# Issuing the first two stores of a streamed elementwise kernel from SyncE instead of GpSimd

## Chip, cores, metric

One core of one Trainium2 chip. The metric is the device time of one execution in microseconds (us), median of several executions. A ratio is the mean time of one kernel's runs over the mean of the other's runs in the same rounds on the same chip, so it is not quite the ratio of the medians that are quoted.

## The reference

```python
# pred, target: (8192, 8192) float32; target is 0.0 or 1.0
def reference(pred, target):
    eps = 1e-7
    pred = np.clip(pred, eps, 1 - eps)
    return -(target * np.log(pred) + (1 - target) * np.log(1 - pred))
```

Two inputs of 268 MB are read and one output of 268 MB is written. As target is 0 or 1, the kernel computes -ln|pred - 1 + target|, one Ln in place of two.

## The kernel before

The inputs are cut into chunks. Per partition there are two of 7680 elements, 32 of 15360, two of 7680 and one of 2048. Two rings in SBUF, one for pred (fp32, worked on in place and stored from there) and one for target (cast to bf16 while it is loaded), hold two large chunks each; chunk 3 lies where chunks 0 and 1 lay. So the load of pred for chunk 3 must wait until the stores of chunks 0 and 1 have landed.

I write pK, tK and sK for the load of pred, the load of target and the store of chunk K. Each of these is 128 rows, one per partition: the 16 DMA engines take 8 rows each. A transfer has landed when the last of its rows is through and its semaphore is up. A transfer that is issued and still waits for the DMA engines is backlog; a stretch in which nothing waits and the DMA engines stand idle is a hole.

```python
    def load(k):
        queue = nc.sync if k == 0 else nc.gpsimd
        nc.gpsimd.dma_start(out=spot(ring_t, k), in_=chunk(target, k))
        queue.dma_start(out=spot(ring_p, k), in_=chunk(pred, k))

    def store(k):
        queue = nc.sync if k >= n - 3 else nc.gpsimd
        queue.dma_start(out=chunk(out, k), in_=spot(ring_p, k))

    def front(k, *part):        # clamp, subtract-and-add on DVE; Abs, Ln on ACT
        ...
    def back(k, *part):         # multiply by -1 on DVE
        ...

        for k in range(3):
            load(k)
        ...
        front(0)
        front(1)
        back(0)
        store(0)
        back(1)
        store(1)
        load(3)
        for k in range(2, n - 4):
            front(k, (0, 2))
            front(k, (1, 2))
            back(k, (0, 2))
            back(k, (1, 2))
            store(k)
            for j in range(k + 2, n if k == n - 5 else k + 3):
                load(j)
        ...   # the last four chunks
```

## Time and profile before

| | before |
|---|---|
| median time | 1866.37 us (3 runs, 1865.87 to 1866.57) |
| span of the profiled run | 1864.1 us |
| DVE, ACT, GpSimd busy | 60%, 48%, 3% |
| DMA engines busy | 100%, nearly all for the GpSimd queue |
| bytes across HBM | 805 MB, 432 GB/s over the span |

How to read it: where the DMA engines are full from end to end and the bytes are fixed, only two things can change the time. One is time in which a DMA engine has nothing to do, the other is rows that take longer than they need. An idle engine elsewhere is not a loss.

### The profile page before, as it was taken

The page shows a single profiled execution, that of the slowest core. Times are in us where ns is not written, and L with a number is a line of the kernel's source. Part 1 is how long each engine was busy: PE and PEld are TensorE (multiplying, and loading weights), DVE is VectorE, ACT ScalarE, POOL GpSimd, SP SyncE. Part 2 cuts the span into 40 slices and gives each one's busy share as a digit, 9 for nine tenths or more (in the row PEclk, how much of TensorE's full clock was granted, in tenths as well). Part 3 has the DMA queues.
Part 4 walks back from the last instruction along what each step waited for, and adds up shares of the span by engine and source line. Part 5 has one row for each costly group of instructions (what it writes and reads, how often), then busy time and mean ns, then how long its engine had stood idle before and what let it go on. Part 6 is the DMA issues. An engine that isn't in the chain of part 4 may idle for free.

```text
span 1864.1 us, 619 instructions
## 1 busy us (share of the span) xinstructions
DVE 1122.2 (60%) x210; ACT 899.9 (48%) x142; POOL 57.5 (3%) x111
## 2 busy tenths in 40 slices
DVE  4655766555576655557665555766555576655585
ACT  3345553335555333555533355553335555333565
POOL 0000000000000000000000000000000000000000
DMA  9999999999999999999999999999999999999999
GB/s 295 374 357 341 353 343 368 383 384 351 347 352 344 371 382 384 348 349 353 347 367 384 382 352 347 353 345 368 385 382 352 345 353 348 365 387 380 353 334 389
DMA packets 15988, 671.13 MB, mean 360 GB/s; under 512 B 1776, under 2 KB 1776, under 8 KB 1904
## 3 DMA queue, kind: packets, MB, share of 16 engines
q0 software_dynamic: 15408, 658.25, 98.5%
q1 hardware_dynamic: 576, 12.85, 1.7%
q14 instruction: 4, 0.03, 0.0%
HBM read 536.87 MB, written 268.44 MB: 432 GB/s over the span
## 4 chain that ended last, share of the span: by engine, by line
DMA 35%; issue 26%; ACT 22%; DVE 15%; POOL 1%; DVEq 0%; POOLq 0%; PEldq 0%
DMA ring_p<-in_pred_dram 32%; ACT ring_p L88 11%; ACT ring_p L89 11%; DVE ring_p L85 7%; DVE ring_p L82 4%; DVE ring_p L93 4%; DMA out_dram<-ring_p 3%; POOL ring_t L73 0%; POOL out_dram L78 0%; DVEq L157 0%; POOL ring_p L74 0%; POOLq L78 0%; POOLq L73 0%; DVEq L82 0%; PEldq L157 0%
## 5 line engine op out<-in xcount | busy, mean ns | idle before, releaser
L88 ACT ACTIVATE ring_p<-ring_p 128x7680 f32<-128x7680 f32 (+1 forms) x70 | 450.6, 6437 | 941.4 <-DVE ring_p L85 941.4
L85 DVE SCALAR_TENSOR_TENSOR ring_p<-ring_t,ring_p 128x7680 f32<-128x7680 bf16 (+1 forms) x70 | 557.2, 7960 | 2.4
L82 DVE TENSOR_SCALAR ring_p<-ring_p 128x7680 f32<-128x7680 f32 (+1 forms) x70 | 284.0, 4057 | 399.0 <-DMA ring_p<-in_pred_dram 399.0
L93 DVE TENSOR_SCALAR ring_p<-ring_p 128x7680 f32<-128x7680 f32 (+1 forms) x69 | 284.0, 4117 | 321.5 <-ACT ring_p L89 321.5
L89 ACT ACTIVATE ring_p<-ring_p 128x7680 f32<-128x7680 f32 (+1 forms) x70 | 451.1, 6444 | 2.2
L74 POOL DMA_DIRECT2D ring_p<-in_pred_dram x36 | 19.3, 535 | 909.2 <-DMA out_dram<-ring_p 909.2
L78 POOL DMA_DIRECT2D out_dram<-ring_p x34 | 18.2, 537 | 851.0 <-DVE ring_p L93 851.0
L73 POOL DMA_DIRECT2D ring_t<-in_target_dram x37 | 20.3, 550 | 0.8 <-PEq L157 0.8
L99 ACT ACT_TABLE_LOAD x1 | 1.3, 1283 | 0.7 <-PEq L146 0.7
L96 DVE MEMSET warm<- 1x8 f32 x1 | 0.1, 65 | 0.8 <-PEq L146 0.8
L99 ACT ACTIVATE warm<-warm 1x8 f32<-1x8 f32 x1 | 0.2, 208 | 0.0
L146 POOL MEMSET const-float32-0.0<- 128x1 f32 x1 | 0.1, 98 | 0.2 <-issue 0.2
L146 POOL MEMSET const-bfloat16-1.0<- 128x1 bf16 x1 | 0.1, 101 | 0.0
L146 POOL MEMSET const-uint8-127<- 128x1 uint8 x1 | 0.1, 99 | 0.0
L146 POOL MEMSET const-float32-1.0<- 128x1 f32 x1 | 0.1, 98 | 0.0
## 6 DMA issues: line engine op xcount, KB each, us to landing
ring_p<-in_pred_dram POOLq DMA_DIRECT2D x32, 7680.0 KB, 35.9
out_dram<-ring_p POOLq DMA_DIRECT2D x32, 7680.0 KB, 29.2
ring_t<-in_target_dram POOLq DMA_DIRECT2D x32, 3840.0 KB, 46.8
ring_p<-in_pred_dram POOLq DMA_DIRECT2D x3, 3840.0 KB, 34.9
ring_t<-in_target_dram POOLq DMA_DIRECT2D x4, 1920.0 KB, 27.7
out_dram<-ring_p POOLq DMA_DIRECT2D x2, 3840.0 KB, 27.6
out_dram<-ring_p SPq DMA_DIRECT2D x2, 3840.0 KB, 15.7
ring_p<-in_pred_dram SPq DMA_DIRECT2D x1, 3840.0 KB, 18.8
```

What stands on the lines that cost most here:

```text
L73: nc.gpsimd.dma_start(out=spot(ring_t, k), in_=chunk(target, k))
L74: queue.dma_start(out=spot(ring_p, k), in_=chunk(pred, k))
L78: queue.dma_start(out=chunk(out, k), in_=spot(ring_p, k))
L82: nc.vector.tensor_scalar(out=p, in0=p, scalar1=EPS, scalar2=1 - EPS, op0=Alu.max, op1=Alu.min)
L85: nc.vector.scalar_tensor_tensor(out=p, in0=t, scalar=1.0, in1=p, op0=Alu.subtract, op1=Alu.add)
L88: nc.scalar.activation(out=p, in_=p, func=Act.Abs)
L89: nc.scalar.activation(out=p, in_=p, func=Act.Ln)
L93: nc.vector.tensor_scalar(out=p, in0=p, scalar1=-1.0, scalar2=None, op0=Alu.mult)
L96: nc.vector.memset(warm, 1.0)
L99: nc.scalar.activation(out=warm, in_=warm, func=Act.Ln)
L146: nc = _bacc.Bacc("TRN2", target_bir_lowering=False, num_devices=1)
```

## The change

The intent: the stores of chunks 0 and 1, which gate p3, should not stand behind p2 in GpSimd's queue, and t3 should not stand behind the stores.

```diff
     def store(k):
-        queue = nc.sync if k >= n - 3 else nc.gpsimd
+        queue = nc.sync if k < 2 or k >= n - 3 else nc.gpsimd
         queue.dma_start(out=chunk(out, k), in_=spot(ring_p, k))
```

## The prediction

> **What bounds the kernel now.** I read the page's first sections, then the transfer issues with the time from issue to landing (for the whole span and for narrow windows around single issues), then the timeline of the first 135 us, and last the single records of the DMA trace. In the page:
>
> ```profile
> DVE 1122.2 (60%) x210; ACT 899.9 (48%) x142; POOL 57.5 (3%) x111
> DMA  9999999999999999999999999999999999999999
> q0 software_dynamic: 15408, 658.25, 98.5%
> q1 hardware_dynamic: 576, 12.85, 1.7%
> HBM read 536.87 MB, written 268.44 MB: 432 GB/s over the span
> ```
>
> No compute engine is busy over 60%, while the two DMA queues fill the time of the 16 DMA engines to 98.5 + 1.7 = 100%. The 805.3 MB that cross HBM are fixed by the reference, so the time is 805.3 MB at about 434 GB/s plus whatever time the DMA engines stand empty. A change in who issues can only add or remove empty time or stalled rows. The chain of waits on the page (stores, loads, ACT and DVE in turn) must be read with that in mind: nearly every wait in it lies under a full DMA queue.
>
> The change touches only the first chunks. The timeline of that stretch:
>
> ```profile
> 52.31 4.15 DVE L93 TENSOR_SCALAR ring_p<-ring_p 128x7680 f32<-128x7680 f32 x1
> 56.76 0.54 POOL L78 DMA_DIRECT2D out_dram<-ring_p  x1 [52.73 <-DVE ring_p L93]
> ...
> 70.15 0.54 POOL L78 DMA_DIRECT2D out_dram<-ring_p  x1 [12.85 <-DVE ring_p L93]
> 70.68 0.55 POOL L73 DMA_DIRECT2D ring_t<-in_target_dram  x1
> 77.39 4.16 DVE L82 TENSOR_SCALAR ring_p<-ring_p 128x7680 f32<-128x7680 f32 x1 [7.54 <-DMA ring_p<-in_pred_dram]
> ...
> 96.16 0.54 POOL L74 DMA_DIRECT2D ring_p<-in_pred_dram  x1 [24.93 <-DMA out_dram<-ring_p]
> ...
> 120.64 0.54 POOL L78 DMA_DIRECT2D out_dram<-ring_p  x1 [23.94 <-DVE ring_p L93]
> ...
> 132.30 4.16 DVE L82 TENSOR_SCALAR ring_p<-ring_p 128x7680 f32<-128x7680 f32 x1 [11.95 <-DMA ring_p<-in_pred_dram]
> ```
>
> I write p2, t2 for the prediction and target loads of chunk 2, s0 for the store of chunk 0, and so on. GpSimd issues s0 at 56.76, s1 at 70.15, t3 at 70.68 and p3 at 96.16, when s1 has landed. One queue serves them in order. With the landing times of those single issues:
>
> ```profile
> out_dram<-ring_p POOLq DMA_DIRECT2D x1, 3840.0 KB, 29.8
> out_dram<-ring_p POOLq DMA_DIRECT2D x1, 3840.0 KB, 25.4
> ring_t<-in_target_dram POOLq DMA_DIRECT2D x1, 3840.0 KB, 43.0
> ring_p<-in_pred_dram POOLq DMA_DIRECT2D x1, 7680.0 KB, 36.1
> ```
>
> the landings are: t2 58.1 (2.93 + 55.2), p2 77.3, s0 86.6, s1 95.6, t3 113.7, p3 132.3. The steps are 19.2, 9.3, 9.0, 18.1 and 18.6 us, which is each transfer's own length: the queue never ran dry. The point to see is that p3, issued at 96.2, still had 17.5 us of t3 ahead of it. This backlog is what hides the wait of p3 for s1. Later, the starts of the first clamp of successive chunks lie 54.3 us apart, and a store is issued 43.2 us after its chunk landed, so 11 us of backlog remain each time.
>
> **What the Trainium skill says.** "DMA: Bandwidth & Descriptors", section Specifications, gives a fabric ceiling of 435 GB/s, and a first byte after about 1 us for transfers issued by GpSimd against 0.6 us from SyncE. The trace agrees with the ceiling (23.59 MB of a chunk in 54.34 us is 434 GB/s); SyncE's first row starts 1.2 us after its issue started (0.74 to 1.98). The same page, section Issuing engines are not separate DMA queues: all issuers run on the same 16 DMA engines, so SyncE adds no bandwidth. Section Queues, rings and completion order: a DMA engine takes turns between its queues packet by packet. The trace confirms this and shows the packet to be one partition row. While p0 (SyncE) and t0 (GpSimd) run together, 7 to 16 us, the rows are nearly equal in number:
>
> ```profile
> q0 software_dynamic: 64, 0.98, 51.2%
> q1 hardware_dynamic: 61, 1.87, 48.8%
> ```
>
> In the records of single rows, each of the 16 DMA engines strictly alternates there. A row of 61,440 B takes 2.267 us, one of 30,720 B read as fp32 1.138 us, and a row of t3 (30,720 B written, twice that read) 2.281 us. Finally, "SBUF — State Buffer", section Who interferes with whom, says that a tensor_scalar in DVE's two-port mode keeps GpSimd off their shared port pair, so that GpSimd cannot write descriptors. No issue in the trace falls into such an instruction, so this is untested here.
>
> **The change part by part.** Removed from GpSimd: two issues of 0.54 us, which cost nothing, as it is 3% busy. Kept: the bytes, and all compute. Three things move.
>
> First, t3 no longer stands behind s0 and s1. It only needs the second DVE pass of chunk 1, ended at 52.4, so it joins GpSimd's queue right behind p2 at the latest after the DVE instruction that ends at 56.5.
>
> Second, s0 and s1 get a queue of their own and alternate row by row with p2 and then t3. On each DMA engine from 58.1 on: GpSimd's queue has 8 rows of p2 and 8 of t3, SyncE's has 8 of s0 and 8 of s1. As s0 comes in one or two rows after p2 started, p2 ends after 8 x 2.267 + 6 or 7 x 1.138 = 25.0 to 26.1 us, near 83.1 to 84.2 instead of 77.3. Chunk 2's compute and s2's issue then move by 6 to 7 us, 120.6 to about 127.5. That is still before p3 ends (132), so it is free.
>
> Third, and this is what costs: s1 (its issue stays at 70.1, its turn comes only after s0, near 87) now finishes together with t3 or a row or two after it. The work is 8 x 2.267 + 8 x 2.281 + 16 x 1.138 = 54.6 us, so all of it is done at 58.1 + 54.6 = 112.7. p3 must wait for s1, landed at 112.7 and no longer at 95.6, and nothing is left in any queue by then. So there is a hole: 0.1 us from last row to landing, 0.55 us from landing to the issue (95.6 to 96.16 before), 0.54 us of issue, then 1.0 us (the skill's first byte) to about 2.9 us. The latter is an estimate from the start, where t0's issue ended at 1.84 and its first row came in the turn that was chosen near 4.7. The sum is 2.2 to 4.1 us, middle 3.1.
>
> To this come first rows of an idle queue, slower by about 0.7 us (1.6 to 2.3 us instead of 1.14 at the start of the kernel; also seen where SyncE's stores begin at the tail, on half of the DMA engines) for p3, and about 0.5 us for s0. Against it stands the stall of p2's last row (up to 3.6 instead of 2.27 us at 73 us, right ahead of s0), worth 1.1 us, which may go. p3 then lands at 112.7 + 0.5 + 3.1 + 0.7 + 18.2 = 135.2 instead of 132.3, so +2.9. From there the period is set by DMA again and nothing gives the loss back. The DMA engines restart in step, and in step the rows ahead of a store stall a little: the periods before were 54.9, 55.6, 54.5, 54.8, 54.4, 54.7, then 54.34, some 3 us in total. I add 0.6 us for having that once more. Sum: +3.5 us on 1866.4, 1869.9 us.
>
> **The rivals.** (a) The intent: stores no longer queue behind loads, p3 is released early, the change gains. If s1 landed near 90, p3 would still queue behind t3, and the best outcome is the removed 1.1 us stall, 1865.3. Against it: s0 must wait for a turn per row, and the bytes before s1's last row grow by t3's.
> (b) Turns by bytes instead of rows. Then s0 would take half the bandwidth, p2 would end near 94, s2's issue would move past 137, and a second hole of 5 to 7 us would open: 1873. The alternation of rows, and the tail, where a 61,440 B row follows each 30,720 B row of SyncE, speak against.
> (c) p3's issue falls into DVE's multiply of chunk 2's first half (103.05 before, so 109 to 114 now) and GpSimd's descriptors wait for it. The issue comes near 113.3, so this costs 0 to 1 us, included in the range; if it hit in full, +4, 1873.
> (d) The hole closes because t3 ends last by a row or two: then +0 to +1, 1867.
>
> **Range and chances.** The hole of 2.2 to 4.1, the stalls of -1.1 to +1.5, and (d) below and (c) above give 1866.8 to 1873.0. All of these lie within 0.5%, while 2% is 37 us. Nothing in the profile could move that much, except a slip in throughput when two queues run side by side, of which the tail shows nothing: 0.005 faster, 0.99 same, 0.005 slower.
>
> **What would show it.** In the profile after: t3 issued near 52 to 57; the first clamp of chunk 2 near 83 to 85; s1 landing some 42 us after its issue, near 113; p3's issue near 113 and its landing only about 20 us later instead of 36.1 (the sign of an empty queue); DMA share under 1.0 in the window from 112 to 118; the clamp of chunk 3 near 135; periods of 54.3 afterwards. It is wrong if s1 lands well before t3, if p3 still takes over 25 us, or if the periods after chunk 3 change.

## The result

| | before | after |
|---|---|---|
| median | 1866.34 us (6 runs) | 1873.52 us (6 runs, 1871.75 to 1874.41) |
| span of the profiled run | 1864.1 us | 1869.9 us |
| ratio | | 1.0038 (95% interval 1.0025 to 1.0050) |

The changed kernel is 7 us slower. By the limit of 2% this is "the same", and the direction and the place were foretold, but the median lies 0.5 us above the stated range, and the loss is twice the 3.5 us of the sum. The profiled execution, 1871.75 us, is the fastest of the six.

The profile after, the timeline of the first chunks (start us, us, engine, line, operation, in brackets the idle time of the engine before it and what ended it):

```profile
52.68 3.90 POOL L73 DMA_DIRECT2D ring_t<-in_target_dram  x1 [48.66 <-DVE ring_p L85]
56.49 13.73 SPq L78 DMA_DIRECT2D out_dram<-ring_p  x2
...
86.12 4.16 DVE L82 TENSOR_SCALAR ring_p<-ring_p 128x7680 f32<-128x7680 f32 x1 [16.26 <-DMA ring_p<-in_pred_dram]
...
111.78 4.16 DVE L93 TENSOR_SCALAR ring_p<-ring_p 128x7680 f32<-128x7680 f32 x1 [1.04 <-ACT ring_p L89]
115.56 0.53 POOL L74 DMA_DIRECT2D ring_p<-in_pred_dram  x1 [58.98 <-DMA out_dram<-ring_p]
...
129.36 0.54 POOL L78 DMA_DIRECT2D out_dram<-ring_p  x1 [13.27 <-DVE ring_p L93]
...
137.83 4.16 DVE L82 TENSOR_SCALAR ring_p<-ring_p 128x7680 f32<-128x7680 f32 x1 [8.77 <-DMA ring_p<-in_pred_dram]
```

Chunk 2 starts at 86.1 (77.4 before), p3 is issued at 115.6 (96.2 before) and chunk 3 starts at 137.8 (132.3 before). The issues of the same stretch, the last column being us from issue to landing:

```profile
ring_t<-in_target_dram POOLq DMA_DIRECT2D x1, 3840.0 KB, 61.1
...
out_dram<-ring_p SPq DMA_DIRECT2D x1, 3840.0 KB, 33.0
...
out_dram<-ring_p SPq DMA_DIRECT2D x1, 3840.0 KB, 45.1
...
ring_p<-in_pred_dram POOLq DMA_DIRECT2D x1, 7680.0 KB, 22.2
```

s1, issued near 69.9, lands at 115.0 (25.4 us after its issue before, 45.1 now), and p3 now lands 22.2 us after its issue instead of 36.1: it found nothing ahead of it. What was a hidden wait has become an empty machine. The same window, 112 to 117 us, in both kernels (length, busy us and instructions of DVE, ACT and POOL, clock, share of DMA time, GB/s; a row counts in the window in which it starts, so a share can exceed 1). Before:

```profile
112.00:117.00 5.00, 0.82 (x1) 4.15 (x1) 0.00 (x0) 1.00 1.14 492
```

After:

```profile
112.00:117.00 5.00, 3.94 (x1) 5.00 (x1) 0.53 (x1) 1.00 0.43 147
```

The DMA share falls to 0.43.

**An account of the time.** The trace records each row that a DMA engine moved, with start and duration. It does not name the engine; where single engines are spoken of below, a row was put on the engine whose last row ended as it began. From these records I worked out two sums for each run, from 50 us on: *empty* (up to 12 us before the end, where the queues run out), the time in which fewer than 16 rows were under way, counted per missing row and divided by 16; and *slow*, what rows took above the usual time of their size (2.267, 2.281, 1.151 or 1.138 us), only where it was over 0.1 us, again divided by 16. If these are the only two ways to lose time, the span less both should be the same in every kernel.

| profiled run | span | empty | slow | span less both |
|---|---|---|---|---|
| before | 1864.1 | 0.1 | 2.4 | 1861.6 |
| after | 1869.9 | 4.4 | 4.1 | 1861.4 |

It is, to 0.2 us. This is bookkeeping: with the same rows to move it must come out, so it says where the time went and not why. Of the 5.8 us between the two profiled runs, 4.3 us are empty DMA engines and 1.7 us are slower rows.

### The profile page after: what moved, and what is told of

It is laid out like the page before. It is cut to its first block, busy times and chain, and to the rows that moved or that the text cites. A ratio compares the mean times of both kernels' runs of the same rounds, so it can differ in the third digit from the quotient of the medians.

```text
span 1869.9 us, 619 instructions
## 1 busy us (share of the span) xinstructions
DVE 1122.2 (60%) x210; ACT 899.9 (48%) x142; POOL 59.8 (3%) x109
## 4 chain that ended last, share of the span: by engine, by line
DMA 33%; ACT 24%; issue 24%; DVE 16%; POOL 1%; another core or an unknown queue 1%; DVEq 0%; POOLq 0%; PEldq 0%
DMA ring_p<-in_pred_dram 32%; ACT ring_p L88 12%; ACT ring_p L89 12%; DVE ring_p L85 8%; DVE ring_p L82 4%; DVE ring_p L93 4%; DMA out_dram<-ring_p 2%; POOL ring_t L73 0%; POOL out_dram L78 0%; DVEq L157 0%; POOLq L78 0%; DVEq L82 0%; PEldq L157 0%
```

## The experiments

Theory 1: the loss is a hole; s1 now ends last together with t3, so p3 is issued when all queues are empty. Theory 2: two queues side by side lose throughput. Theory 3: GpSimd cannot write the descriptors of p3 while DVE multiplies. Eleven runs were made. The kernel before that they are compared with had medians of 1866.0 to 1866.2 us beside them.

| run | median us (runs) | ratio to before | 95% interval | span | empty | slow | span less both |
|---|---|---|---|---|---|---|---|
| a_again (the change) | 1873.76 (5) | 1.0040 | 1.0028 to 1.0053 | 1871.1 | 4.4 | 4.9 | 1861.8 |
| a_third (the change) | 1873.93 (1) | | | 1872.1 | 3.9 | 6.0 | 1862.2 |
| b_s0_only | 1868.34 (5) | 1.0011 | 0.9998 to 1.0025 | 1866.5 | 0.1 | 4.0 | 1862.4 |
| c_s1_only | 1866.24 (5) | 1.0000 | 0.9987 to 1.0012 | 1863.8 | 0.1 | 2.4 | 1861.4 |
| d_t3_halves | 1867.67 (5) | 1.0011 | 0.9998 to 1.0023 | 1865.6 | 0.1 | 3.9 | 1861.6 |
| d0_before_t3_halves | 1866.03 (5) | 0.9999 | 0.9986 to 1.0011 | 1864.6 | 0.1 | 2.7 | 1861.8 |
| e_mult_act | 1872.37 (5) | 1.0033 | 1.0020 to 1.0045 | 1870.3 | 3.7 | 5.0 | 1861.5 |
| h_hole_only | 1871.71 (5) | 1.0028 | 1.0015 to 1.0042 | 1869.8 | 2.9 | 5.0 | 1861.9 |
| x_t3_late | 1873.12 (5) | 1.0039 | 1.0027 to 1.0052 | 1870.5 | 4.9 | 4.3 | 1861.3 |
| f_p3_first | 1872.03 (5) | 1.0033 | 1.0020 to 1.0047 | 1869.9 | 3.6 | 4.6 | 1861.7 |
| g_mid_sp | 1949.38 (4) | 1.0446 | 1.0431 to 1.0460 | 1946.9 | 52.4 | 32.2 | 1862.4 |

The last column stays between 1861.3 and 1862.4 us while the spans run from 1863.8 to 1946.9. The account closes, so the question for each run is only how much it was empty, how much slow, and why. Row times below are counted from the program's first instruction, as the issue times are. All results were correct.

### The change again (a_again, a_third)

The edit is a comment, so that the same kernel gives a second and a third trace.

> The changed kernel once more, for a second trace and for its spread. Theory 1 (a hole: p3 waits for s1, which now lands last, and all queues are empty meanwhile): 1872 to 1874.5 us, and in the trace p3's first row starts 1.5 to 3 us after the last row of s1, p3 lands 20 to 23 us after its issue. Theory 2 (two queues side by side lose throughput, row by row): the same time, but the loss is then in rows longer than 1.14 and 2.27 us between 58 and 113 us. Theory 3 (GpSimd cannot write p3's descriptors while DVE multiplies chunk 2): the issue of p3 takes up to 4 us, not 0.54, in the slower runs.

> The changed kernel a third time, one look at its trace. The two traces so far have chunk 3's first clamp at the same 137.83 us though their times differ by 1.2 us. If the spread of the changed kernel comes from later stalls, chunk 3's clamp is again at 137.5 to 138.2 us whatever the time, and the periods after it differ. If it comes from the hole, the clamp moves with the time.

Measured: 1872.16 to 1874.51 us in five runs, and a single one of 1873.93 us (its state is unknown, so it serves for its trace only). The signs of Theory 1 are there: in all three traces p3's first row starts 2.2 us after the last row of s1, and p3 lands 22.2 us after its issue. Those of the others are not: between 58 and 113 us the slow rows are 1.0 to 1.1 us, against 1.0 in the kernel before, and p3's issue takes 0.53 us each time. Chunk 3's first clamp starts at 137.83 us in the first two traces and at 137.37 us in the third (just under the 137.5 to 138.2 expected), which is the slowest of the three. From there to the start of chunk 33's clamp the three take 1633.15, 1634.41 and 1635.79 us (before: 1632.84). So the spread of these three traces comes from slow rows after the hole, not from the hole. That the slower runs without a trace had more slow rows too is likely from this, not shown. Of the spans' differences from before, 5.8, 7.0 and 8.0 us, the empty part is 4.3, 4.3 and 3.8 us, the slow part 1.7, 2.5 and 3.6 us.

### One store alone (b_s0_only, c_s1_only)

```diff
-        queue = nc.sync if k < 2 or k >= n - 3 else nc.gpsimd
+        queue = nc.sync if k < 1 or k >= n - 3 else nc.gpsimd     # b_s0_only
+        queue = nc.sync if k == 1 or k >= n - 3 else nc.gpsimd    # c_s1_only
```

> Only s0 goes to SyncE; s1 stays with GpSimd, ahead of t3. Theory 1: s1 lands near 95 us with all of t3 still queued behind it, so there is no hole; 1866 to 1868 us, no more than the stalled rows beside s0 are worth. Theory 2: about half of the time with two queues remains, so about half of the loss, 1869.5 to 1870.5 us. Theory 3: p3's issue comes near 95 us, beside DVE's subtract-and-add pass or its clamp; no loss or up to 4 us hidden under t3: 1866.5 us.

> Only s1 goes to SyncE; s0 stays with GpSimd, ahead of t3. Theory 1: s1 alternates with the end of p2 and with s0 and lands near 94 us, before t3; no hole: 1866 to 1868 us. Theory 2: about half of the loss, 1869.5 to 1870.5 us. Theory 3: as for s0 alone, 1866.5 us.

Measured: 1868.34 us, just over the range of Theory 1 and under that of Theory 2, and 1866.24 us, inside Theory 1's (and near the 1866.5 us of Theory 3). In both, s1 lands near 95 us with t3 behind it, and nothing is ever empty. p3's issues, first with s0 alone, then with s1 alone, again us to landing in the last column:

```profile
ring_p<-in_pred_dram POOLq DMA_DIRECT2D x1, 7680.0 KB, 36.5
```

```profile
ring_p<-in_pred_dram POOLq DMA_DIRECT2D x1, 7680.0 KB, 36.1
```

They find the backlog that the kernel before had (36.1 us). So the loss is not half for half the change: only both stores together let s1 end last. With s0 alone there are 1.6 us of slow rows more than before. Its interval just reaches 1, so this 2 us is likely but not clear; it came without a hole.

### Keep the change, fill the hole (d_t3_halves), with its control (d0_before_t3_halves)

DMA engines take turns by rows, so t3 in shorter rows lasts for more turns. t3 is loaded as two halves of the columns:

```diff
     def load(k):
         queue = nc.sync if k == 0 else nc.gpsimd
-        nc.gpsimd.dma_start(out=spot(ring_t, k), in_=chunk(target, k))
+        if k == 3:
+            h = widths[k] // 2
+            for i in range(2):
+                nc.gpsimd.dma_start(
+                    out=spot(ring_t, k, (i, 2)), in_=chunk(target, k)[:, i * h : (i + 1) * h]
+                )
+        else:
+            nc.gpsimd.dma_start(out=spot(ring_t, k), in_=chunk(target, k))
```

d_t3_halves has it on the changed kernel, d0_before_t3_halves on the kernel before.

> Both stores on SyncE as in the change, but t3 is loaded as two transfers of half the columns, so that GpSimd's queue has 16 short rows of t3 in place of 8 long ones and is not through with them when s1 ends. Turns by rows then let s1 land near 104 us (8 rows of p2, 8 half rows of t3, 16 rows of stores after 58 us) with 9 us of t3 left. Theory 1: the hole is gone, p3 lands 27 us or so after its issue, 1866.5 to 1868.5 us. Theory 2: as much time with two queues as in the change, 1872 to 1874 us. Theory 3: p3's issue now falls beside the subtract-and-add pass[...]; the loss is gone as well, so this run does not part 1 from 3.

> A control: the kernel before, its stores of the first two chunks on GpSimd, with t3 loaded as two halves. If the halves only fill the hole, they do nothing here: 1865.5 to 1867 us under each theory. If it were faster by 1 us or more, the gain of the halves in the changed kernel would not be the hole's.

Measured: 1867.67 us, 6 us less than the change, and the control 1866.03 us, no change. p3's issue and landing, and then the DMA share from 104 to 109 us, with the halves in the changed kernel:

```profile
107.01 0.53 POOL L81 DMA_DIRECT2D ring_p<-in_pred_dram  x1 [50.54 <-DMA out_dram<-ring_p]
```

```profile
ring_p<-in_pred_dram POOLq DMA_DIRECT2D x1, 7680.0 KB, 25.5
```

```profile
104.00:109.00 5.00, 5.00 (x1) 4.97 (x2) 0.53 (x1) 1.00 1.03 218
```

p3 is issued at 107.0 with 5 to 7 us of t3 still queued, by DMA engine, which covers the 1.2 us that p3 took in the change from its issue to its first row, and the empty part goes from 4.4 to 0.1 us. Both stores still go through SyncE and still alternate with p2 and t3. So this run shows that some 6 of the 7 us go with the hole and not with the two queues. What is left, 1.7 us over before, is again slow rows (3.9 against 2.4), as with s0 alone; its interval, too, reaches 1. The part of the expectation that put the landing at about 27 us was close (25.5); s1 landed at 106.4 and not near 104; the time for Theory 2 (1872 to 1874) failed.

### The hole by itself, in one queue (h_hole_only)

The kernel before, with p3 held back until t3 has landed (`probe` is a spare tile of 8 elements; its declaration is left out here and in x_t3_late):

```diff
         nc.gpsimd.dma_start(out=spot(ring_t, k), in_=chunk(target, k))
+        if k == 3:
+            nc.gpsimd.tensor_copy(out=probe, in_=spot(ring_t, 3)[0:1, 0:8])
         queue.dma_start(out=spot(ring_p, k), in_=chunk(pred, k))
```

> The kernel before, with one thing added: GpSimd copies 8 elements of t3 to a spare tile ahead of p3's issue, so p3 is issued only when t3 has landed (near 113.7 us) and all queues are empty. No second queue is in use. Theory 1: the hole alone makes most of the loss: first row of p3 about 2.2 us after t3's landing, first rows 0.7 us slow, a last-row stall of about 1 us as the DMA engines restart in step; 1869.5 to 1871.5 us. Theory 2 (side-by-side queues): no loss, 1866 to 1867 us.

Measured: 1871.71 us, 5.5 us above before, slightly over the top of the expectation. The timeline, and the DMA share of the window:

```profile
113.33 0.18 POOL L76 COPY probe<-ring_t 1x8 bf16<-1x8 bf16 x1 [42.25 <-DMA ring_t<-in_target_dram]
113.86 0.54 POOL L77 DMA_DIRECT2D ring_p<-in_pred_dram  x1 [0.35 <-issue]
```

```profile
112.00:117.00 5.00, 1.23 (x1) 3.73 (x1) 0.72 (x2) 1.00 0.57 197
```

In the row records t3's last row ends at 112.95 us and p3's first one starts at 115.1 us. The hole is 2.9 us per DMA engine, and the slow rows grow from 2.4 to 5.0 us though no second queue is in use. So emptying the queues once costs twice: the hole itself, and nearly as much in slow rows afterwards. For these 2.6 us the prediction had 0.7 us (p3's first rows) and 0.6 us (rows stalled later).

### DVE's multiply away from p3's issue (e_mult_act)

```diff
-            back(k, (0, 2))
+            if k == 2:
+                p = spot(ring_p, k, (0, 2))
+                nc.scalar.mul(out=p, in_=p, mul=-1.0)
+            else:
+                back(k, (0, 2))
             back(k, (1, 2))
```

> The changed kernel, with the multiply of chunk 2's first half given to ACT, after the Ln of the second half. DVE is then idle when p3 is issued, and s2 is issued near 131 to 132 us, still before p3 has landed (137.8). Theory 1 (hole): p3 is issued 0.6 us after s1 landed, as before; 1872 to 1874.5 us. Theory 3 (p3's descriptors wait for DVE's multiply): 1 to 3 us less, 1870 to 1872.5 us.

Measured: 1872.37 us, inside both ranges, so the time does not decide. The trace says more: from s1's last row to p3's issue there are 0.93 to 0.94 us in this run, in all three traces of the change and in the kernel before, and from that issue to the first row 1.23 us both here and in the profiled run after. Theory 3 has nothing to explain in these traces. But it is not void: see the next run.

### t3 issued late (x_t3_late)

```diff
         store(1)
+        nc.gpsimd.tensor_copy(out=probe, in_=spot(ring_p, 1)[0:1, 0:8])
         load(3)
```

> Both stores on SyncE, but GpSimd reads 8 elements of chunk 1 after its multiply, ahead of t3's issue, so t3 is issued near 70.6 us as in the kernel before and not at 52.7. Theory 1: what counts is t3's place in the queue, right behind p2, and p2 runs until 85 us either way; the hole stays, p3 is issued near 115 us, 1871.5 to 1874.5 us. Rival (the early issue of t3, held 3.9 us by DVE, does the harm): 1866 to 1868 us.

Measured: 1873.12 us, so the early issue is harmless: what counts is that t3 stands right behind p2, with no store between. The trace:

```profile
70.07 0.53 POOL L74 DMA_DIRECT2D ring_t<-in_target_dram  x1 [0.31 <-issue]
...
112.28 4.16 DVE L94 TENSOR_SCALAR ring_p<-ring_p 128x7680 f32<-128x7680 f32 x1 [1.04 <-ACT ring_p L90]
...
115.28 1.28 POOL L75 DMA_DIRECT2D ring_p<-in_pred_dram  x1 [44.68 <-DMA out_dram<-ring_p]
```

p3's issue takes 1.28 us here in place of 0.53 and ends 0.1 us after DVE's multiply, which runs until 116.44. "SBUF — State Buffer", section Who interferes with whom, of the Trainium skill has descriptors held up by DVE's two-port mode, in which DVE also takes the ports that it shares with GpSimd, and the issue of t3 in the change agrees: it took 3.90 us in place of 0.55 beside a DVE multiply that ended 0.1 us before it. So Theory 3 fits an effect of 0.75 us in this one trace, though no run took the multiply away here, and this trace's empty part is the largest of its kind, 4.9 us.

### p3 ahead of t3 (f_p3_first)

```diff
     def load(k):
         queue = nc.sync if k == 0 else nc.gpsimd
+        if k == 3:
+            queue.dma_start(out=spot(ring_p, k), in_=chunk(pred, k))
+            nc.gpsimd.dma_start(out=spot(ring_t, k), in_=chunk(target, k))
+            return
```

> Both stores on SyncE, and p3 issued ahead of t3. s1 then follows s0 with nothing beside it once p2 has ended, lands near 95 us, and p3 is issued near 95.7 with all queues empty: a hole as long as in the change, only 20 us earlier. Theory 1: 1869.5 to 1873 us, the first row of p3 some 2 us after s1's landing, and t3, not p3, the load that chunk 3 waits for, near 135 to 137 us. Rival (taking turns with t3 as such is the cost): no rows of t3 beside a store, so 1866.5 to 1868.5 us.

Measured: 1872.03 us. s1 has the DMA engines to itself once p2 is done and lands at 95.6 us, as early as in the kernel before. The issues of p3 and t3:

```profile
96.26 0.54 POOL L74 DMA_DIRECT2D ring_p<-in_pred_dram  x1 [92.24 <-DMA out_dram<-ring_p]
96.78 0.55 POOL L75 DMA_DIRECT2D ring_t<-in_target_dram  x1
```

p3 is issued as early as before, at 96.3, and it lands 20.7 us later: the queue was empty again, only 20 us sooner. The time is lost all the same (empty 3.6, slow 4.6), so the rival, that taking turns with t3 as such is the cost (1866.5 to 1868.5), failed. An early landing of the store that gates a load is worth nothing by itself; work queued behind that store is.

### The later stores on SyncE (g_mid_sp)

```diff
-        queue = nc.sync if k >= n - 3 else nc.gpsimd
+        queue = nc.gpsimd if k < 2 else nc.sync
```

> The first two stores on GpSimd as before, and all the later ones on SyncE. In each chunk the store then takes turns with the end of the next prediction load and the start of the next target load; by rows of equal length it is through some 2 rows (4 us) ahead of the target load, so the next prediction load is issued just in time. Theory 1: no hole in the mean, short ones on the DMA engines that run ahead: 1866 to 1880 us. Theory 2 (side by side loses throughput): 30 times the 1.5 to 2 us of the two early stores, 1910 to 1930 us.

Measured: 1949.38 us, 83 us slower, and both ranges missed. The account splits it into 52.3 us of empty DMA engines and 29.8 us of slow rows. My working of the steady state (a store ends two rows ahead of the target load, each time) did not hold. What the trace shows is a cycle of two chunks, with an empty stretch in it:

```profile
1022.28 0.53 POOL L74 DMA_DIRECT2D ring_p<-in_pred_dram  x1 [52.17 <-DMA out_dram<-ring_p]
1022.81 0.54 POOL L73 DMA_DIRECT2D ring_t<-in_target_dram  x1
...
1072.35 0.53 POOL L74 DMA_DIRECT2D ring_p<-in_pred_dram  x1 [49.00 <-DMA out_dram<-ring_p]
1078.57 0.53 POOL L73 DMA_DIRECT2D ring_t<-in_target_dram  x1 [5.70 <-DVE ring_p L85]
```

```profile
1016.00:1026.00 10.00, 1.35 (x1) 9.97 (x2) 1.06 (x2) 1.00 0.70 270
1080.00:1090.00 10.00, 3.48 (x1) 9.97 (x2) 0.00 (x0) 1.00 1.02 442
```

At 1022 us a prediction load is issued when its store has landed, and the DMA share around it is 0.70: the target load ended before the store that gates the next load. At 1072 us it is issued with a backlog. So the harm of the change repeats where stores and loads sit in two queues, about 5 us for every two chunks (83 us over the 32 stores that moved). The row records show 16 empty stretches, one about every 114 us from 221 us on, of 2.3 to 4.4 us each. They also show where the slow rows are: in the mean of 14 such cycles 2.0 of 2.1 us start within 15 us after the emptying, and 0.1 us in the other 99 us, in which stores and loads take turns as well. (Half of the 2.0 us comes 10 to 15 us after the emptying, where the next store begins.) So here the slow rows come with the emptying, as in h_hole_only, and not from the two queues as such.

## Why the prediction was wrong in size and right in place

**Right:** what bounds the kernel (the DMA engines are 100% busy before, and what the profiled run lost is empty and slow DMA time); the turns by rows; p2 landing later (86 us measured, 83 to 85 foretold); t3 right behind p2; s1 landing with the end of t3; p3 issued into empty queues (22.2 us to landing, "about 20" foretold); the later start of chunk 2 and of s2 being free; no gain from the intent. Rival (b), turns by bytes, and rival (d), a hole that closes, did not occur. The mechanism, a hole because s1 lands last, was right. What failed are sizes. One is the slow rows, above all in the two slower traces: their terms (0.5 for s0, 0.7 for p3's first rows, 0.6 for rows in step, less the stall of 1.1) add up to 0.7 us, and they measured 1.7 to 3.6 us. The other is the hole, set at 3.1 us and measured at 3.8 to 4.3.

**The landing of s1.** The prediction had "all of it is done at 58.1 + 54.6 = 112.7" and 0.5 us for slow first rows, 113.2. In the three traces s1's last row ends at 114.6, 114.7 and 114.2, and it lands 0.35 us later (115.0, 115.0, 114.6). The sum treated the 16 DMA engines as one. In their mean it was right: s1's rows end at 112.7 to 112.8. But s1 has landed when the last of them is through. In the profiled run the first of them ends s1 at 112.1 us and the last at 114.6, a spread of 2.5 us (2.5 and 1.9 in the other two), against 1.0 us at 58 us; in the kernel before, the 16 parts of t3 land within 1.25 us of each other at the same place. The faster ones stand empty meanwhile. This is why the empty part is 4.4 us per DMA engine and not the 3.1 in the middle of the sum. Why the spread grows there is not shown.

**The start of p3.** "0.1 us from last row to landing, 0.55 us from landing to the issue", then the issue, "then 1.0 us (the skill's first byte) to about 2.9 us". Measured: 0.35, 0.58 and 0.53 us, and 0.70 us from the end of the issue to the first row (116.80). So the skill's 1 us was near (1.23 us if counted from the start of the issue), and the 2.9 us that I read off the kernel's start was not. From s1's last row to p3's first is 2.2 us where the sum's middle had 3.1. This error hid part of the first, which is luck. The prediction also put its row times 0.24 us late against the issues: SyncE's first row starts at 1.75 us and not 1.98, 1.0 us after its issue and not 1.2.

**The slow rows.** The first rows of p3 took 2.3 to 3.3 us (0.6 us extra in the mean, foretold 0.7). "I add 0.6 us for having that once more" is the term that failed most. In the profiled run after, p3's last row on each of the 16 DMA engines took 3.1 to 4.2 us instead of 2.27, which alone is 1.2 us in the mean, and over all three traces the slow rows grew by 1.7 to 3.6 us against before, the removed stall at 73 us already counted. The median of the change, 1.8 us above its profiled run, fits the upper part of that. h_hole_only shows that a hole in a single queue brings 2.6 us of them too.

**Rival (c)** is small: 0.75 us in x_t3_late, nothing visible in the profiled run. (Its "+4, 1873" is a slip: 1869.9 and 4 give 1873.9.)

Left open: why rows slow down. In the traces they come in bunches, on most of the 16 DMA engines at once, in the last row of a prediction load ahead of a store, and fewer of them as the engines drift apart. That they come from engines being in step is a reading of the order of events; no run changed the step alone. Also open is why b_s0_only and d_t3_halves have 1.5 to 1.6 us more of them than the kernel before without a hole: both have s0 on SyncE, c_s1_only has not and shows none. How much of the slow rows of the change is of this kind is not parted.

No version beat the kernel before; c_s1_only and d0_before_t3_halves equal it.

## What to carry to other kernels

On a kernel whose DMA engines are full, the position of a transfer in the queue is part of its schedule: ask of each load that waits for a store what is still queued when that store lands, and keep at least the restart (2.2 us here), plus the spread of the DMA engines (2.5 us here), behind it. A second issuing queue added no bandwidth here, it only made rows take turns, so a store moved there can end later than in its old place (45 us in place of 25). And emptying the queues once cost about twice the hole (5.5 us for 2.9 us in h_hole_only).

## What the Trainium skill lacked or had wrong

- "DMA: Bandwidth & Descriptors", section Issuing engines are not separate DMA queues, says that issuing from several engines saves only sequencer time, and that the transfers interleave. It lacks what that can cost: a store that takes turns with a load can land later than in its old place. Two stores moved from GpSimd to SyncE cost 7 us, all later ones 83 us; section Issuing engine by pattern puts plain stores on SyncE without such a reserve.
- The same page, section SWDGE vs HWDGE vs iDMA, gives a packet, the unit at which a DMA engine changes queues, as preferably up to 4096 B. Here the unit of a turn was a whole row, up to 61,440 B and 2.27 us.
- The same page, section Specifications, gives the first byte of a GpSimd transfer as about 1 us, but not from where it is counted: with empty queues the first row started 0.70 us after the end of the issue, 1.23 us after its start.
- No page has the slow rows after queues ran empty: in the change last rows of p3 of 3.1 to 4.2 us in place of 2.27, and 2.6 us more in total in h_hole_only.
